# Every second weight piece of the experts issued from ScalarE's queue instead of SyncE's, with the overflow branch and the first preloaded pieces moved

## The chip, the cores and the metric

The kernel runs on one core of one Trainium2 chip. The metric is the device time of one execution in microseconds (us). TensorE (PE) multiplies, VectorE (DVE), ScalarE (ACT) and GpSimd (POOL) work elementwise, and SyncE (SP) does nothing but issue DMAs. Any of ACT, POOL and SP can issue a DMA. All matrices come from HBM as float32 and are read once: 418.78 MB in all.

## The reference

Two residual layers over 256 rows of 1024. The second ends in a top-2-of-8 expert SwiGLU, whose weights are most of the bytes (8 experts of 44 MB):

```python
def moe_swiglu(x, router, w_gate, w_up, w_down):
    logits = (t @ router).astype(jnp.float32)
    top_logits, top_idx = lax.top_k(logits, TOP_K)
    top_w = jax.nn.softmax(top_logits, axis=-1)
    ...
    for e in range(N_EXPERTS):
        out = out + gates[:, e:e + 1] * swiglu(t, w_gate[e], w_up[e], w_down[e])
```

The first layer (convolution, pooling, dense SwiGLU) and the first half of the second (short convolution, spatial gating) take 60 MB of weights.

## The kernel before, in words

Weights arrive in **pieces** ("chunks") of 1 MB, numbered in the order of use. The list `chunks` holds 57 pieces for everything ahead of the experts, then 336 for the experts. `raw_half` (L114) allocates a buffer and issues the piece's load the first time that it is asked for; the issue waits until the buffer's last reader is done. There are 8 general buffers (`raw`), and during a while some more that other data leave free (`AHEAD`, and the `whi` and `wlo` buffers by `IN_HI` and `IN_LO`, which name pieces by number).

The **experts** are taken by load: position 0 is a fixed expert, positions 1 to 7 are ranked on the chip, and their number is read into a register. Each position has a capacity in rows (`CAPS`): positions 1, 2 and 3 have 128 or more and are here called wide, the others 64 and are called plain. For wide positions each half of a piece is rounded by ACT into `whi` (L151) and the remainder is made by DVE into `wlo` (L158), both before PE may use it; PE then runs three passes. For plain positions PE multiplies by the raw piece itself. Position 1 has 32 rows beside its 128.

Each position runs through 7 **passes**; `STARTS` says in which pass it begins. Pass by pass the work is a list of **items**: gate, up and down of each position in the pass, two pieces each, so 6 pieces for each position in a pass. By `STARTS`, passes 0 to 3 and 25 to 27 hold one plain position, passes 4 to 10 and 18 to 24 one wide and one plain (12 pieces), and passes 11 to 17 one wide and two plain (18 pieces). In a pass of two or more the order is gates, then the downs of the pass before, then ups. Below, gW, dW and uW are the gate, down and up item of the wide position of such a pass, and gP, dP and uP those of the plain one: the order is gW gP dW dP uW uP.

The order on every engine is the order in which the code is written. `use` (L177) calls `prep`, which asks for the piece two ahead of the one that PE is to use (`LOOK_HI` = 4 halves). At an item's first step the results of the item before are taken from PSUM by ACT (`fdk`, `sgate`, L1298: a wait for PE) ahead of that. Because SP has no other work, it stands at a wait for a buffer and runs ahead of all other engines as far as there are free buffers.

Near the end, at item `end - IF_AT`, all engines read a flag and branch around code for rows over capacity (`over_capacity`, L1459), which isn't taken here. Ahead of it all pieces that are left have been asked for.

Of the kernel before, what the change touches and what calls it, by code (L numbers as in the profile page):

```python
# [8 lines left out]
F32 = mybir.dt.float32  # L9
# [8 lines left out]
P = 128  # L18
T = 256
# [4 lines left out]
NE = 8  # L24
# [8 lines left out]
RAW_BUFS = 8  # L33
WAIT = (6, 12, 6, 2)
CARRY = {(1, 0): 1, (1, 1): 2, (0, 0): 3, (0, 1): 3}
IF_AT = 5
CARRY_AT = 1
LAST_CUT = 2
AHEAD = {"ft": (0, 50), "fd": (15, 24), "fa": (2, 18), "fc": (3, 48), "fe": (7, 50), "fb": (8, 56), "f0": (9, 18), "f1": (10, 60)}

IN_HI, IN_LO = (16, 17, 18, -7, -6, -5), (19, 20, -4, -3)
TAIL, TAIL_HI, TAIL_LO = 12, 2, 1
RANK_AT = 3
FILL = (5, 2, 5, 4)
# [31 lines left out]
def tile_trunk(ctx: ExitStack, tc: tile.TileContext, a: dict, out: bass.AP, caps=CAPS, starts=STARTS,  # L76
               stop=None, dump=None):
    nc = tc.nc
    te, ve, se, pe_, sy = nc.tensor, nc.vector, nc.scalar, nc.gpsimd, nc.sync
# [21 lines left out]
    chunks, slot_pools = [], {"ra": rawp}  # L101
    raws, his, los, ahead = {}, {}, {}, {}
    state = {"use": 0}
# [7 lines left out]
    def block_chunk(w, r0, c0):  # L111
        chunks.append((lambda: w[r0:r0 + 512, c0:c0 + 512].rearrange("(k p) f -> p k f", p=P), 4, 512))

    def raw_half(n):  # L114

        c, h = divmod(n, 2)
        src, k, f = chunks[c]
        if c in ahead and ahead[c] in ("whi", "wlo"):
            if c not in raws:
                pool = hip if ahead[c] == "whi" else lop  # L120
                raws[c] = [pool.tile([P, k // 2, f], F32, name=ahead[c]) for _ in range(2)]
                for i, r in enumerate(raws[c]):
                    sy.dma_start(r, src()[:, i * k // 2:(i + 1) * k // 2, :])
            return raws[c][h]
        if c not in raws:
            tag = ahead.get(c, "raw")
            raws[c] = slot_pools[tag[:2]].tile([P, k, f], F32, name="raw", tag=tag)
            v = src()
            if c < FIRST_CUT:
                for i in range(2):  # L130
                    sy.dma_start(raws[c][:, :, i * P:(i + 1) * P], v[:, :, i * P:(i + 1) * P])
            elif c < len(chunks) - LAST_CUT:
                sy.dma_start(raws[c], v)
            else:
                for i in range(2):
                    sy.dma_start(raws[c][:, i * k // 2:(i + 1) * k // 2, :], v[:, i * k // 2:(i + 1) * k // 2, :])
        return raws[c][:, :, h * P:(h + 1) * P] if k == DB else raws[c][:, h * k // 2:(h + 1) * k // 2, :]

    spare = []
    made = {"hi": 0, "lo": 0}  # L140
# [55 lines left out]
    fg, fu, fd = a["even_ffn_w_gate"][0], a["even_ffn_w_up"][0], a["even_ffn_w_down"][0]  # L196
    o_in, o_out = a["odd_w_in"][0], a["odd_w_out"][0]
    mg, mu, md = a["odd_moe_w_gate"][0], a["odd_moe_w_up"][0], a["odd_moe_w_down"][0]
    eid_reg = {}
# [25 lines left out]
    n_moe = 2 * len(chunks)  # L225
# [7 lines left out]
    for c in range(max(c1 for _, c1 in AHEAD.values())):  # L233
        if c in IN_HI + IN_LO:
            continue
        tag = min((v[0], t) for t, v in held_by.items() if t == "raw" or AHEAD[t][0] <= c < AHEAD[t][1])[1]
        held_by[tag] = held_by[tag][1:] + [c]
# [13 lines left out]
    for p, n0 in starts:  # L251
        kept = [(m, k) for m, k in kept if m + NFB > n0]
        spills[p] = []
        for _, n in _blocks(caps[p]):
            k = 2 if n == P else 1
# [5 lines left out]
        plan.insert(len(plan) - 2, plan.pop(len(plan) - 5))  # L261

    def expert(p, w, r0, nr, c0, ncol):
        def src():
            if p and p not in eid_reg:
                eid_reg[p] = sy.value_load(ctli[0:1, p:p + 1], min_val=0, max_val=NE - 1)
            if p == 0:
                v = w[0, r0:r0 + nr, c0:c0 + ncol]
            else:
                v = w[bass.ds(eid_reg[p], 1), r0:r0 + nr, c0:c0 + ncol].rearrange("o r f -> (o r) f")  # L270
            return v.rearrange("(k p) f -> p k f", p=P)
        chunks.append((src, nr // P, ncol))

# [8 lines left out]

    for tag, cs in (("whi", IN_HI), ("wlo", IN_LO)):
        for c in cs:
            ahead[c + (n_moe // 2 if c > 0 else len(chunks))] = tag

    def stay_warm(n, w, m=None):

# [418 lines left out]
    for pair in range(2):  # L707
        for h in range(2):
            s = ws3(use())
# [14 lines left out]
    for q in range(4):  # L724
        w = use_plain() if PLAIN_B else use()
        for t in range(2):
            for j in range(2):
                k = 2 * q + j
# [15 lines left out]
    for g in range(4):  # L744
        o = bs[g // 2][:, (g % 2) * T:(g % 2 + 1) * T]
# [10 lines left out]
    for g in range(4):  # L756
        o = bs[g // 2][:, (g % 2) * T:(g % 2 + 1) * T]
# [100 lines left out]
    fe = ctx.enter_context(tc.tile_pool(name="fe", bufs=1, side="right"))  # L858
# [34 lines left out]
    fa = fy.tile([P, 2, 1024], F32, name="fa")  # L893
    fb = fy.tile([P, 2 * 1024 + 4], F32, name="fb")
    fc = fy.tile([P, 4, 512], F32, name="fc")
# [44 lines left out]
    for pair in range(2):  # L940
        for h in range(2):
            w = use()
            j = 2 * pair + h
            s = combine(ws_tile(w, x2T))
# [3 lines left out]
    for pair in range(2):  # L948
        for h in range(2):
            w = use()  # L950
            combine(ws_tile(w, x2T), vT[:, 2 * pair + h, :])
    for n in range(2):
# [3 lines left out]
        s = fc[:, 3, :]  # L956
# [7 lines left out]
    for pair in range(2):  # L964
        for h in range(2):
            w = use()
            j = 2 * pair + h
            s = combine(ws_tile(w, x2T))
# [7 lines left out]
    for pair in range(2):  # L976
        for h in range(2):
            w = use()
            j = 2 * pair + h
            s = combine(ws_tile(w, x2T))  # L980
# [92 lines left out]
    mop = ctx.enter_context(tc.tile_pool(name="mop", bufs=2, reuse_waits="tile"))  # L1073
# [25 lines left out]
    ctli = cst([P, NE + 1], "ctli", I32)  # L1099
# [122 lines left out]
    sgate, mh = {}, {}  # L1222
# [236 lines left out]
    def over_capacity():  # L1459

        R = total[0]
        flag = nc.values_load(ctli[0:1, NE:NE + 1], min_val=0, max_val=1)
        with tc.If(flag > 0):  # L1463
            capE, over = cst([P, NE], "capE"), cst([P, 2, NE], "over")
            c = small.tile([P, NE, NE], F32, name="bypos", bufs=1)
            ve.tensor_tensor(c, oh, capt[:, :, None].to_broadcast(sq), op=OP.mult)
            ve.tensor_reduce(capE, c.rearrange("p a e -> p e a"), axis=AX.X, op=OP.add)
            for t in range(2):
                ve.tensor_tensor(over[:, t, :], s1[:, t, :], capE, op=OP.is_gt)
            ve.tensor_tensor(over, over, gates, op=OP.mult)  # L1470
            xf = fx.tile([P, DB, T], F32, name="xf", tag="f0")
            for t in range(2):
                for q in range(2):
                    b = bank()
                    for k in range(4):
                        te.transpose(b[:, k * P:(k + 1) * P], X[:, t, (4 * q + k) * P:(4 * q + k + 1) * P], ident)
                    se.activation(xf[:, 4 * q:4 * q + 4, t * P:(t + 1) * P], b.rearrange("p (k f) -> p k f", k=4),
                                  AF.Copy)
            for e in range(NE):
                with tc.For_i(0, FE, P) as f0:  # L1480
                    wgu = fy.tile([P, 2, DB, P], F32, name="fbgu", tag="fc")
                    for i, w in enumerate((mg, mu)):
                        sy.dma_start(wgu[:, i], w[e][:, bass.ds(f0, P)].rearrange("(k p) f -> p k f", p=P))
                    wdt = fx.tile([P, D], F32, name="fbd", tag="f1")
                    sy.dma_start(wdt, md[e][bass.ds(f0, P), :])
                    bs = [bank(), bank()]
                    for i in range(2):
                        for k in range(DB):
                            mm(bs[i][:, :T], wgu[:, i, k, :], xf[:, k, :], k == 0, k == DB - 1)
                    s = mop.tile([P, T], F32, name="fbh", tag="mh", bufs=2)  # L1490
                    se.activation(s, bs[0][:, :T], AF.Silu)
                    ve.tensor_tensor(s, s, bs[1][:, :T], op=OP.mult)
                    for t in range(2):
                        for h in range(2):
                            sl = slice(h * 512, (h + 1) * 512)
                            b = bank()
                            mm(b, s[:, t * P:(t + 1) * P], wdt[:, sl], True, True)
                            ve.scalar_tensor_tensor(R[:, t, sl], b, over[:, t, e:e + 1], R[:, t, sl], op0=OP.mult,
                                                    op1=OP.add)
# [9 lines left out]
    for n, item in enumerate(plan):  # L1509
        if n == RANK_AT:  # L1510
            ranking()
        if n == total_at:
            start_total()
        if item in gathers:
            later(1, gather, *gathers[item])
        if n == end - IF_AT:
            drain()
            for c in range(made["hi"] // 2, len(chunks)):
                raw_half(2 * c)
            over_capacity()  # L1520
        if n == end - CARRY_AT:
            for (t, h), d in CARRY.items():
                if d < 4:
                    later(d, carry, t, h)
        if n >= end:
            drain()
        if n == len(plan) - 1:
            for (t, h), d in CARRY.items():
                if d >= 4:
                    later(d - 3, carry, t, h)  # L1530
        if item[0] == "d":
            down(*item[1:])
        else:
            project(*item)
# [19 lines left out]
    for t in range(2):  # L1554
        for h in range(2):
            nb = len(blocks[last])
            for bi in range(nb):
                if (t, h) not in F:
                    F[t, h] = bank()
                y, r = (ysum[last, bi][h], slice(0, P)) if blocks[last][bi][1] == P else \  # L1560
# [18 lines left out]
    for t in range(2):  # L1579
        for h in range(2):  # L1580
            r = y[:, t, half(h)]
# [33 lines left out]
```

## Time and profile before

| | us |
|---|---|
| median of 2 timed runs (1315.39 to 1319.24) | 1317.32 |
| the profiled execution | 1314.88 |
| its span, first to last instruction | 1313.2 |
| PE busy in it | 1256.2 |
| DVE busy | 713.5 |
| ACT busy | 514.5 |

The profiled execution lies 2.4 us under the median and 1.7 us over its own span. PE's busy time is modelled and counts pipelined matmuls, so a stage with a busy PE can still be one that waits for data. For that the DMA columns of the time slices are read.

### The profile page before, as it was taken

The page shows a single profiled execution, that of the slowest core. Times are in us where ns is not written, and L with a number is a line of the kernel's source. Part 1 is how long each engine was busy: PE and PEld are TensorE (multiplying, and loading weights), DVE is VectorE, ACT ScalarE, POOL GpSimd, SP SyncE. Part 2 cuts the span into 40 slices and gives each one's busy share as a digit, 9 for nine tenths or more (in the row PEclk, how much of TensorE's full clock was granted, in tenths as well). Part 3 has the DMA queues.
Part 4 walks back from the last instruction along what each step waited for, and adds up shares of the span by engine and source line. Part 5 has one row for each costly group of instructions (what it writes and reads, how often), then busy time and mean ns, then how long its engine had stood idle before and what let it go on. Part 6 is the DMA issues. An engine that isn't in the chain of part 4 may idle for free. (4 is left out here: it accounts for less than half of the span.)

```text
span 1313.2 us, 19384 instructions
## 1 busy us (share of the span) xinstructions
PE 1256.2 (96%) x7585; PEld 871.1 (66%) x7585; DVE 713.5 (54%) x1105; ACT 514.5 (39%) x726; POOL 32.0 (2%) x69
## 2 busy tenths in 40 slices
PE   7989999999999999999999999999999999999875
PEld 6848888888777666667765566565556567665541
DVE  4897676667984244655534334434435565564313
ACT  4246555546442144544432233332333244454200
POOL 5000000001000001000000000000000000000000
PEclk8999999999999999999999999999999999999988
DMA  8425755176875999999999999999999999999991
GB/s 293 166 70 176 256 184 182 65 253 194 323 271 185 393 393 394 394 392 393 393 393 371 381 397 374 364 380 391 392 397 396 394 393 395 393 394 394 393 393 76
DMA packets 195884, 421.17 MB, mean 321 GB/s; under 512 B 6896, under 2 KB 43448, under 8 KB 195784
## 3 DMA queue, kind: packets, MB, share of 16 engines
q1 hardware_dynamic: 194280, 414.58, 85.2%
q0 software_dynamic: 1504, 5.28, 1.1%
q8 instruction: 61, 1.00, 0.3%
q14 instruction: 39, 0.32, 0.1%
HBM read 418.78 MB, written 1.05 MB: 320 GB/s over the span
## 5 line engine op out<-in xcount | busy, mean ns | idle before, releaser
L158 DVE TENSOR_TENSOR wlo<-raw,whi 128x1024 fp32r<-128x1024 f32 x354 | 417.8, 1220 | 175.8 <-ACT whi L151 159.1
L151 ACT ACTIVATE whi<-raw 128x1024 fp32r<-128x1024 f32 x354 | 354.6, 1050 | 215.7 <-DMA raw<-in_odd_moe_w_up 99.1
L98 PE MATMUL mm<-whi,xgw 128*128 128x512 f32 x672 | 215.9, 403 | 0.4 <-DVE total L1431 0.4
L98 PEld LDWEIGHTS mm<-whi,xgw 128*128 128x128 f32 x672 | 122.0, 189 | 44.6 <-issue 13.3
L98 PE MATMUL mm<-raw,f1k 128*64 128x256 f32 (+1 forms) x1344 | 133.9, 384 | 0.0
L98 PE MATMUL mm<-wlo,xgw 128*128 128x512 f32 x336 | 131.9, 392 | 0.3 <-DVE wlo L158 0.3
L98 PE MATMUL mm<-big,whi 128*128 128x512 f32 (+1 forms) x448 | 129.2, 368 | 2.5 <-ACT whi L151 1.8
L98 PE MATMUL mm<-raw,fek 128*64 128x256 f32 x880 | 106.6, 390 | 7.3 <-DVEq L1463 6.7
L98 PE MATMUL acc<-whi,mh 128*128 128x512 f32 x336 | 106.3, 397 | 1.7 <-ACT whi L151 1.7
L98 PEld LDWEIGHTS mm<-raw,f1k 128*64 128x64 f32 (+1 forms) x1344 | 72.7, 127 | 52.2 <-issue 17.4
L1298 ACT ACTIVATE fdk<-mm 128x256 f32<-128x256 f32 (+1 forms) x49 | 23.2, 474 | 182.1 <-PE mm L98 181.9
L98 PE MATMUL mm<-big,wlo 128*128 128x256 f32 x384 | 92.7, 283 | 0.0
L98 PEld LDWEIGHTS mm<-raw,fek 128*64 128x64 f32 x880 | 61.1, 139 | 45.5 <-issue 19.0
L1301 DVE TENSOR_TENSOR fdk<-mm,fdk 128x256 f32<-128x256 f32 (+1 forms) x49 | 26.3, 537 | 118.5 <-PE mm L98 118.5
L98 PEld LDWEIGHTS mm<-big,whi 128*128 128x128 f32 x448 | 74.9, 192 | 14.2 <-ACT whi L151 2.0
L98 PE MATMUL acc<-raw,fbs 128*64 128x512 f32 (+1 forms) x528 | 84.0, 507 | 0.0
L98 PEld LDWEIGHTS acc<-whi,mh 128*128 128x128 f32 x336 | 61.4, 188 | 24.4 <-ACT whi L151 11.0
L98 PEld LDWEIGHTS mm<-wlo,xgw 128*128 128x128 f32 x336 | 63.5, 189 | 14.9 <-DVE wlo L158 0.7
L98 PEld LDWEIGHTS mm<-big,wlo 128*128 128x128 f32 x384 | 69.3, 192 | 3.7
L98 PE MATMUL acc<-wlo,mh 128*128 128x512 f32 (+1 forms) x176 | 67.8, 401 | 0.5 <-DVE wlo L158 0.5
L98 PEld LDWEIGHTS acc<-raw,fbs 128*64 128x64 f32 (+1 forms) x528 | 26.6, 125 | 47.9 <-issue 44.9
L98 PE MATMUL acc<-whi,ffh 128*128 128x512 f32 x176 | 55.6, 396 | 0.0
(292 smaller groups left out, 1315.7 us busy)
## 6 DMA issues: line engine op xcount, KB each, us to landing
raw<-in_odd_moe_w_gate SPq DMA_DIRECT2D x110, 1024.0 KB, 13.8
raw<-in_odd_moe_w_up SPq DMA_DIRECT2D x109, 1024.0 KB, 13.9
raw<-in_odd_moe_w_down SPq DMA_DIRECT2D x105, 1024.0 KB, 12.8
raw<-in_even_ffn_w_gate SPq DMA_DIRECT2D x11, 1024.0 KB, 5.6
raw<-in_even_ffn_w_up SPq DMA_DIRECT2D x11, 1024.0 KB, 8.3
raw<-in_even_ffn_w_down SPq DMA_DIRECT2D x11, 1024.0 KB, 7.0
raw<-in_odd_w_in SPq DMA_DIRECT2D x10, 1024.0 KB, 15.2
raw<-in_even_w_in SPq DMA_DIRECT2D x5, 1024.0 KB, 8.8
```

Of the source, the lines that this page charges most:

```text
L98: te.matmul(o, lhsT, rhs, start=start, stop=stop)
L151: se.activation(his[n], r, AF.Copy)
L158: ve.tensor_tensor(los[n], r, his[n].bitcast(F32), op=OP.subtract)
L1298: se.activation(s, v, AF.Silu)
L1301: ve.tensor_tensor(s, v, s, op=OP.mult)
```

## The change

- Pieces of the experts with an odd number (the first of each item's two, since the first expert piece is number 57) are issued by ACT (`se`) instead of SP. The order of the calls stays. Both engines read an expert's number into a register of their own.
- The branch is at 10 items ahead of the end instead of 5, and ahead of it pieces are asked for up to 8 past the one in use, not all that are left.
- Of the first pieces, 15 to 17 go to `whi` and 18 and 19 to `wlo` buffers (before: 16 to 18, and 19 and 20), the last pieces no longer use such buffers, and the buffer `fd` takes pieces from number 20 on instead of 15.
- A scratch tile in the branch's code shares another buffer.

```diff
-IF_AT = 5
+IF_AT = 10
...
-AHEAD = {"ft": (0, 50), "fd": (15, 24), ...
+AHEAD = {"ft": (0, 50), "fd": (20, 24), ...
-IN_HI, IN_LO = (16, 17, 18, -7, -6, -5), (19, 20, -4, -3)
+IN_HI, IN_LO = (15, 16, 17), (18, 19)
...
+    def raw_queue(c):
+
+        return se if c >= n_moe // 2 and c % 2 else sy
...
+                v = src()
                 for i, r in enumerate(raws[c]):
-                    sy.dma_start(r, src()[:, i * k // 2:(i + 1) * k // 2, :])
+                    raw_queue(c).dma_start(r, v[:, i * k // 2:(i + 1) * k // 2, :])
...
             elif c < len(chunks) - LAST_CUT:
-                sy.dma_start(raws[c], v)
+                raw_queue(c).dma_start(raws[c], v)
...
-            for c in range(made["hi"] // 2, len(chunks)):
+            for c in range(made["hi"] // 2, state["use"] // 2 + RAW_BUFS):
                 raw_half(2 * c)
```

ACT in a pass with one wide and one plain position, before: roundings (`whi`) and results taken from PSUM (`fdk` of 512 columns is the wide gate's, of 256 the plain gate's; `mh` is a transposed up).

```order
L435 ACTIVATE mh<-mm 128x4x128
L151 ACTIVATE whi<-raw 128x1024 x2
L1298 ACTIVATE fdk<-mm 128x512
L151 ACTIVATE whi<-raw 128x1024 x4
L1298 ACTIVATE fdk<-mm 128x256
L151 ACTIVATE whi<-raw 128x1024 x6
L435 ACTIVATE mh<-mm 128x4x128
```

The same place now, from the load of gP's first piece on; the ISA rows set the register for the address.

```order
L138 DMA raw<-in_odd_moe_w_gate 128x4x512
L1306 ACTIVATE fdk<-mm 128x512
L138 ISA
L138 DMA raw<-in_odd_moe_w_down 128x2x1024
L157 ACTIVATE whi<-raw 128x1024 x4
L1306 ACTIVATE fdk<-mm 128x256
L138 ISA
L138 DMA raw<-in_odd_moe_w_down 128x2x1024
L138 ISA
L138 DMA raw<-in_odd_moe_w_up 128x4x512
L157 ACTIVATE whi<-raw 128x1024 x4
```

The load of dW's first piece now stands behind the taking of the wide gate's result, and right ahead of the roundings of that same piece; the loads of dP's and uW's first pieces stand behind these and behind the plain gate's result.

SP from the third piece of position 0 on, before: both pieces of an item, one after the other.

```order
L133 DMA raw<-in_odd_moe_w_up 128x4x512 x2
L133 DMA raw<-in_odd_moe_w_gate 128x4x512 x2
L133 DMA raw<-in_odd_moe_w_up 128x4x512 x2
L133 DMA raw<-in_odd_moe_w_down 128x2x1024 x2
L133 DMA raw<-in_odd_moe_w_gate 128x4x512 x2
L133 DMA raw<-in_odd_moe_w_up 128x4x512 x2
L133 DMA raw<-in_odd_moe_w_down 128x2x1024 x2
L123 DMA whi<-in_odd_moe_w_gate 128x2x512 x4
```

ACT at the start of the experts now; `sgate` takes the result of position 0's gate from PSUM.

```order
L1306 ACTIVATE sgate<-mm 128x256
L138 DMA raw<-in_odd_moe_w_gate 128x4x512
L138 DMA raw<-in_odd_moe_w_up 128x4x512
L1306 ACTIVATE sgate<-mm 128x256
L138 DMA raw<-in_odd_moe_w_down 128x2x1024
L138 DMA raw<-in_odd_moe_w_gate 128x4x512
L138 DMA raw<-in_odd_moe_w_up 128x4x512
L1306 ACTIVATE sgate<-mm 128x256
L138 DMA raw<-in_odd_moe_w_down 128x2x1024
L128 DMA whi<-in_odd_moe_w_gate 128x2x512 x2
L128 DMA wlo<-in_odd_moe_w_up 128x2x512 x2
L1306 ACTIVATE sgate<-mm 128x256
```

The odd pieces of position 0 now stand behind the taking of PE's results, three after each gate; before, nothing of PE's expert work stood ahead of them on their queue but the buffers.

## Rows read from the trace of the kernel before

**Rows 1.** The page: 40 equal slices of the span, DMA busy tenths and rate.

```profile
DMA  8425755176875999999999999999999999999991
GB/s 293 166 70 176 256 184 182 65 253 194 323 271 185 393 393 394 394 392 393 393 393 371 381 397 374 364 380 391 392 397 396 394 393 395 393 394 394 393 393 76
```

**Rows 2.** Windows: stretch, length, busy PE, PEld, DVE, ACT, POOL, clock, DMA share, GB/s.

```profile
400.00:420.00 20.00, 20.00 (x170) 14.70 (x171) 12.06 (x41) 4.25 (x10) 0.00 (x0) 1.00 0.26 92
560.00:620.00 60.00, 60.00 (x343) 40.54 (x343) 33.33 (x37) 27.41 (x33) 0.00 (x0) 1.00 1.04 394
```

**Rows 3.** The page, costliest groups: DVE's and ACT's making of `wlo` and `whi`.

```profile
L158 DVE TENSOR_TENSOR wlo<-raw,whi 128x1024 fp32r<-128x1024 f32 x354 | 417.8, 1220 | 175.8 <-ACT whi L151 159.1
L151 ACT ACTIVATE whi<-raw 128x1024 fp32r<-128x1024 f32 x354 | 354.6, 1050 | 215.7 <-DMA raw<-in_odd_moe_w_up 99.1
```

**Rows 4.** Timeline of PE and ACT, one pass of a wide and a plain position.

```profile
574.85 3.67 PE L98 MATMUL mm<-raw,fek 128*64 128x256 f32 x32
578.45 0.73 PE L98 MATMUL acc<-whi,mh 128*128 128x512 f32 x2
...
584.11 3.65 PE L98 MATMUL acc<-raw,fbs 128*64 128x512 f32 x16
...
574.96 0.60 ACT L1298 ACTIVATE fdk<-mm 128x512 f32<-128x512 f32 x1 [6.17 <-PE mm L98]
...
582.68 2.01 ACT L151 ACTIVATE whi<-raw 128x1024 fp32r<-128x1024 f32 x2 [3.07 <-DMA raw<-in_odd_moe_w_up]
```

**Rows 5.** Timeline of PE, a gate item of position 1: first and last instructions.

```profile
765.07 1.07 PE L98 MATMUL mm<-raw,f1k 128*32 128x256 f32 x16
...
771.78 4.67 PE L98 MATMUL mm<-raw,f1k 128*32 128x256 f32 x48
```

**Rows 6.** Source line L133, SP's issues: ns min/median/max; landing over all of its pieces.

```profile
L133 SPq DMA_DIRECT2D raw<-in_even_ffn_w_gate x11: 367/368/368, 28.1 to 261.3; - x11
...
DMA to landing us min/median/max: 4.8/13.0/19.1
```

**Rows 7.** Source line L1540, two loads of 512 KB from POOL's queue beside SP's.

```profile
L1540 POOL DMA_DIRECT2D lnf<-in_odd_ln_g x1: 587/587/587, 992.5 to 992.5; - x1
L1540 POOL DMA_DIRECT2D lnf<-in_odd_ln_b x1: 531/531/531, 993.1 to 993.1; - x1
...
DMA to landing us min/median/max: 6.6/7.4/8.1
```

**Rows 8.** ACT's sequencer (ACTq) at the branch, and ACT's instruction ahead of it.

```profile
L1462 ACTq TENSOR_LOAD <-ctli x1: 467/467/467, 1260.4 to 1260.4; - x1
...
1260.42 0.39 ACT L1298 ACTIVATE fdk<-mm 128x256 f32<-128x256 f32 x1 [2.39 <-PE mm L98]
```

**Rows 9.** Timeline of SP, then of ACT, where the experts begin.

```profile
384.77 29.32 SPq L133 DMA_DIRECT2D raw<-in_odd_moe_w_down  x2
414.18 2.09 SPq L123 DMA_DIRECT2D whi<-in_odd_moe_w_gate  x4
...
429.48 0.39 ACT L1298 ACTIVATE sgate<-mm 128x256 f32<-128x256 f32 x1 [10.47 <-PE mm L98]
440.33 0.39 ACT L1298 ACTIVATE sgate<-mm 128x256 f32<-128x256 f32 x1 [10.47 <-PE mm L98]
```

**Rows 10.** Timeline of PE behind the branch.

```profile
1268.25 6.89 PE L98 MATMUL mm<-raw,fek 128*64 128x256 f32 x40 [6.75 <-DVEq L1463]
1275.07 0.44 PE L1308 MATMUL mm<-ident,fdk 128*128 128x128 f32 x2
```

More of the change, by code (lines that the diff above doesn't have):

```diff
@@ L35 @@
 CARRY = {(1, 0): 1, (1, 1): 2, (0, 0): 3, (0, 1): 3}
-IF_AT = 5
+IF_AT = 10
 CARRY_AT = 1
 LAST_CUT = 2
-AHEAD = {"ft": (0, 50), "fd": (15, 24), "fa": (2, 18), "fc": (3, 48), "fe": (7, 50), "fb": (8, 56), "f0": (9, 18), "f1": (10, 60)}
-IN_HI, IN_LO = (16, 17, 18, -7, -6, -5), (19, 20, -4, -3)
+AHEAD = {"ft": (0, 50), "fd": (20, 24), "fa": (2, 18), "fc": (3, 48), "fe": (7, 50), "fb": (8, 56), "f0": (9, 18), "f1": (10, 60)}
+IN_HI, IN_LO = (15, 16, 17), (18, 19)
 TAIL, TAIL_HI, TAIL_LO = 12, 2, 1
@@ L132, in raw_half @@
             elif c < len(chunks) - LAST_CUT:
-                sy.dma_start(raws[c], v)
+                raw_queue(c).dma_start(raws[c], v)
             else:
                 for i in range(2):
-                    sy.dma_start(raws[c][:, i * k // 2:(i + 1) * k // 2, :], v[:, i * k // 2:(i + 1) * k // 2, :])
+                    raw_queue(c).dma_start(raws[c][:, i * k // 2:(i + 1) * k // 2, :],
+                                           v[:, i * k // 2:(i + 1) * k // 2, :])
         return raws[c][:, :, h * P:(h + 1) * P] if k == DB else raws[c][:, h * k // 2:(h + 1) * k // 2, :]
@@ L263, in expert @@
     def expert(p, w, r0, nr, c0, ncol):
+        on = raw_queue(len(chunks))
         def src():
-            if p and p not in eid_reg:
-                eid_reg[p] = sy.value_load(ctli[0:1, p:p + 1], min_val=0, max_val=NE - 1)
+            if p and (p, on) not in eid_reg:
+                eid_reg[p, on] = on.value_load(ctli[0:1, p:p + 1], min_val=0, max_val=NE - 1)
             if p == 0:
@@ L269, in src @@
             else:
-                v = w[bass.ds(eid_reg[p], 1), r0:r0 + nr, c0:c0 + ncol].rearrange("o r f -> (o r) f")
+                v = w[bass.ds(eid_reg[p, on], 1), r0:r0 + nr, c0:c0 + ncol].rearrange("o r f -> (o r) f")
             return v.rearrange("(k p) f -> p k f", p=P)
@@ L284, in tile_trunk @@
         for c in cs:
-            ahead[c + (n_moe // 2 if c > 0 else len(chunks))] = tag
+            ahead[n_moe // 2 + c] = tag
     def stay_warm(n, w, m=None):
@@ L1489, in over_capacity @@
                             mm(bs[i][:, :T], wgu[:, i, k, :], xf[:, k, :], k == 0, k == DB - 1)
-                    s = mop.tile([P, T], F32, name="fbh", tag="mh", bufs=2)
+                    s = mop.tile([P, T], F32, name="fbh", tag="sgate", bufs=1)
                     se.activation(s, bs[0][:, :T], AF.Silu)
```

## The prediction

> **What bounds the kernel now.** I read the page's time slices first, then windows by stage, then the timeline of one pass on PE, ACT and SP. The reader is to see two halves. Up to about 420 us the DMA engines have room and PE sets the pace. From there to 1280 us they move 364 to 397 GB/s, mostly over 390 [rows 1]: 394 GB/s at a DMA share of 1.04 in the window from 560 us, while PE, too, counts as busy all the time [rows 2]. A piece of 1.049 MB so takes 2.67 us, and the passes last what their bytes last: 6 pieces 16 us, 12 pieces 32 us, 18 pieces 48 us. PE's own work is close under this. A wide item takes 5.7 us (578.45 to 584.11) and a plain one 3.7 us [rows 4], so a pass of both has 3 x 9.4 = 28 us; a gate of position 1 takes 765.07 to about 772.8, 7.7 us [rows 5], so a pass with it has 3 x (7.7 + 3.7 + 3.7) = 45 us.
>
> So no second queue can add bytes per second after 420 us. What it can do is to lose the lead. SP has the lead because it waits for nothing but buffers. ACT waits for PE: it sat idle 6.17 us for the wide gate's result before it took it, and 3.07 us for a landing before a rounding [rows 4].
>
> **The issue itself.** SP needs 0.37 us for one where its queue is not full [rows 6]. With ACT it is 168 issues, 62 us in all, beside 515 us of busy time, so ACT's sum of work bounds nothing. What counts is where each stands.
>
> Does a load on ACT's queue wait for what stands ahead of it there? The trace of before has no DMA on ACT. The nearest row is the branch: the read of the flag by ACT's sequencer starts at 1260.4, and the instruction ahead of it, which had waited 2.39 us for PE, at 1260.42 [rows 8]. So it came through when that wait ended, not earlier, and not after the instruction's 0.39 us either. I take it that a load on ACT waits for the *waits* ahead of it, not for the *work*.
>
> The Trainium skill says it otherwise (Perfetto Trace Analysis, DVE / Act Engine Instruction): the sequencer can fetch the next instruction as soon as one is pushed into the wait queue, so a load could be issued past roundings and results that still wait. By that rule the lead would mostly stay; that is rival A. The row above doesn't agree with it for the one control instruction that it shows.
>
> **How long a piece takes to land.** Alone 4.8 us, the least of all of SP's pieces [rows 6]. Beside SP's full queue, two loads of 512 KB from POOL's queue were issued at 992.5 and 993.1 and the later took 8.1 us, so this megabyte was there 8.7 us after its first issue [rows 7], less than the 13.0 us median on SP's own queue [rows 6]: another queue gets a share and doesn't stand behind SP's. Each further piece ahead of it on the same queue costs 2.67 us at the full rate and 5.3 us at half. So one piece lands in 4.8 to 8.7 us, the second of two in 7.5 to 14.0, the third of three in 10.1 to 19.3. Full rate holds when SP's buffers are all filled, half when SP always has something queued. SP is at most 8 buffers ahead and works in ACT's gaps as well, so I take a little under the middle: 6.5, 10 and 13 us.
>
> The Trainium skill (DMA: Bandwidth & Descriptors, Issuing engines are not separate DMA queues) states that loads from several engines interleave on the same 16 DMA engines, and that only issue time is saved. That speaks against a gain, and the 394 GB/s from one queue agree.
>
> **A pass of a wide and a plain position** (passes 4 to 10 and 18 to 24, 14 of them). I count from the landing of gW's first piece. ACT rounds it (1.05 us), DVE makes `wlo` (1.22 us) [rows 3], and PE starts at 2.3 and ends gW at 8.0. The load of gP's first piece went out shortly after 0 and is there in time. ACT then passes its wait for gW's result and issues dW's at 8.3; it lands at 14.8. The load of dP's, and behind it uW's, stand behind the rounding of dW's, which waits for that landing, and behind gP's result (8.0 + 3.7 = 11.7, earlier): out at 15.3. uW's lands 10 us later, 25.3. Behind its rounding go uP's and the next gW's: out at 25.8, landed at 35.8. So the pass lasts 8.3 + 6.5 + 10 + 10 + 1.0 for issues = 35.8 us instead of 32. PE, with 28 us of work, is never later than that. Ends: 8.3 + 4.8 + 7.5 + 7.5 + 1.0 = 29.1, under the 32 us that the bytes need, so no loss; and 8.3 + 8.7 + 14 + 14 + 1.0 = 46 us, 14 more. Sum: 14 x 3.8 = 53 us (0 to 196).
>
> **A pass with position 1 and two plain ones** (passes 11 to 17, 7 of them). From the landing of the wide gate: PE ends it at 10.0, the first plain gate at 13.7, and behind that result the wide down is issued at 13.9. One more plain piece is ahead of it, so it lands at 13.9 + 6.5 + 1 = 21.4. Both plain downs and the wide up go out by 22.5, and the up lands at 22.5 + 13 = 35.5. PE runs downs from 23.7 to 38.9 (7.7 + 3.7 + 3.7), then the wide up to 46.6. The last plain up and the next wide gate are issued behind that up's results, at 47 and 48.5 (the transposed up, `mh`, in between), and the gate lands at 48.5 + 6.5 + 1.5 = 56.5. Instead of 48 that is 8.5 us more; with the shortest landings 2.6, with the longest 19. Sum: 7 x 8.5 = 60 us (18 to 133).
>
> **The start of the experts.** Position 0 alone goes at PE's pace before, 440.33 - 429.48 = 10.85 us a pass [rows 9], faster than the 16 us that 6 pieces take, because SP had loaded some 20 pieces by then. ACT now has 3 odd pieces behind each gate's result. The first, a down, lands 6.5 us after the gate, while the up ahead takes PE only 3.7: some 3 us lost a pass, and the first gate of wide weights later by what ACT's list adds. I take 4 passes x 3 = 12 us (5 to 25; the top is ten odd pieces x 2.67 us, all the lead on ACT's side). The single-position passes at the end need 16 us for their bytes, and 1 + 6.5 + 2 x 3.7 us between a gate's result and the next gate's, so they lose nothing.
>
> **The moved pieces and the branch.** SP stood 29 us up to 414 us in two issues, the second a wait for the buffer `fd`, with `whi` pieces right behind [rows 9], at 92 GB/s [rows 2]. Piece 15 no longer waits for `fd`, which helps SP's side alone; I price it with the start above. The branch cost PE 6.75 us, in a stretch in which PE ran without a gap afterwards [rows 10]. At the start of pass 25 bytes are short, so most of the wait falls beside loads: 5 us won (7 won to 8 lost, if SP's and ACT's own halt at the branch empties the queues). The other buffer of the scratch tile is in code that isn't run: nothing.
>
> **Sum.** 1314.9 + 12 + 53 + 60 - 5 = 1435 us. The profiled execution lies 2.4 us under the median; I leave it at 1435.
>
> **Rivals.** *A: the lead stays.* ACT's sequencer goes past waiting results, or the shortest landings hold. Then a load on ACT stops only for the landing of a wide piece ahead of it, three times a pass, and the passes stay at 32 and about 50 us: 14 x 1 + 7 x 2 + 22 for the lost lead at the start - 5 = +45, 1360 us, and with the shortest landings throughout (0 + 18 + 5 - 7) 1331 us. For it: PE is idle little today, so there is slack for just-in-time loads; against it: the flag's read [rows 8]. *B: a load waits also for the work ahead of it,* or finds SP's queue mostly full. Four roundings (4 x 1.05) stand ahead of each of three issues on the path in a wide pass; 21 passes x 3 x some 2 us that nothing else hides = +126, 1560 us. For it: nothing in the trace excludes it for a load; against: the 0.39 us that the flag's read did not wait. *C: faster.* The mechanism is SP's wait at the start: with half of the pieces on another queue, a piece held up by its buffer no longer holds up those behind it, and the idle 20 us from 400 (92 of 393 GB/s, so 15 us of DMA time) are filled; it decides if ACT then keeps pace everywhere. With 6.75 us from the branch: 1315 - 22 = 1293 us. Against it: ACT's loads at that place stand behind `sgate` results that come only every 10.85 us [rows 9].
>
> **How the numbers follow.** The forecast has 0.62, A 0.19, B 0.14, C 0.05. About 2% (26 us, so under 1291 or over 1341) is what a measurement of this kernel can tell from no change. Faster by more: 0.03, since even C hardly reaches it. Within: 0.15, the lower part of A and most of C. Slower: 0.82. The sum's ends, all at once, are 1314.9 + 16 = 1331 and 1314.9 + 196 + 133 + 25 + 8 = 1677, but all ends at once are unlikely: landings can't all be long when the DMA engines have gaps. The range of 8 in 10 takes most of A and half of B: 1340 to 1560.
>
> **What would show it.** In the trace of the changed kernel: between 450 and 1250 us the rate is some 10% under 393 GB/s, with tenths of 8 in the DMA slices; ACT's landing waits ahead of `whi` grow from 159 us in DVE's column and PE shows real gaps ahead of wide items; ACT's loads start within 1 us of the `fdk` ahead of them; a wide and plain pass lasts about 36 us. If ACT's loads start while a result ahead of them still waits, A holds. If landings on ACT's queue are near 4.8 us, the sum is too high; if they are near 13 us, as on SP's today, it is far too low. The forecast is wrong altogether if the rate stays at 393 GB/s.

## The result, and the profile after

The changed kernel takes **1584.13 us** (1582.86 to 1585.41), 1.2045 times the time before, with an interval of 1.2013 to 1.2077: 267 us slower. The prediction had 1435 us and a range up to 1560, so its direction held and its size did not.

The page of the kernel after shows the same matmuls as before (7585), busy for longer, and DMA slices mostly with tenths of 6 to 8 where [rows 1] has nines. First the engine line, then the DMA lines of the 40 slices.

```profile
PE 1347.7 (85%) x7585; PEld 908.1 (57%) x7585; DVE 713.4 (45%) x1105; ACT 511.8 (32%) x726; POOL 31.8 (2%) x69
...
DMA  9137644576598887888778758686868979889983
GB/s 315 67 107 266 207 139 160 167 259 212 198 377 327 323 291 275 312 322 294 282 266 308 288 199 292 220 313 237 320 261 292 354 279 328 307 328 354 342 319 130
```

The reader is to see that no engine became full: TensorE is busy for 85% of the span, against 96% before, and the rate lies near 300 GB/s, against 393. The costliest groups of the page say what is waited for; they answer to [rows 3]. VectorE's wait for `whi` ahead of `wlo` is 428.3 us instead of 159.1. ScalarE's idle time ahead of `whi` is 485.8 us instead of 215.7, of which the landings of expert pieces are 441 us instead of 149 (gates, ups and downs added up):

```profile
L164 DVE TENSOR_TENSOR wlo<-raw,whi 128x1024 fp32r<-128x1024 f32 x354 | 417.6, 1222 | 450.4 <-ACT whi L157 428.3
L157 ACT ACTIVATE whi<-raw 128x1024 fp32r<-128x1024 f32 x354 | 352.0, 1048 | 485.8 <-DMA raw<-in_odd_moe_w_gate 152.5
```

To see where the time went, I cut both traces at the same events, ScalarE's takings of the 21 results of wide gates (`fdk` of 512 columns): up to the first one, the seven passes of wide and plain positions, the seven passes with position 1, the second block of six such intervals up to the last wide gate, and the rest. Columns: stretch, length, busy PE, PEld, DVE, ACT, POOL, clock, DMA share, GB/s. Before:

```profile
0.00:461.68 461.68, 441.08 (x2477) 357.32 (x2479) 316.71 (x628) 211.82 (x350) 25.00 (x63) 0.99 0.62 216
461.68:678.39 216.71, 214.97 (x1246) 146.63 (x1250) 113.45 (x122) 93.68 (x114) 5.89 (x4) 1.00 1.04 394
678.39:1015.90 337.51, 330.40 (x2390) 201.63 (x2394) 143.19 (x180) 111.80 (x146) 1.12 (x2) 1.00 1.02 384
1015.90:1210.00 194.10, 191.50 (x1040) 123.34 (x1041) 106.45 (x120) 78.44 (x92) 0.00 (x0) 0.99 1.04 394
1210.00:1313.20 103.20, 78.25 (x444) 42.13 (x444) 33.73 (x56) 18.77 (x25) 0.00 (x0) 0.92 0.77 292
```

After:

```profile
0.00:476.83 476.83, 446.22 (x2475) 357.77 (x2475) 317.18 (x628) 211.52 (x350) 24.85 (x63) 0.97 0.60 207
476.83:754.42 277.59, 234.43 (x1246) 154.60 (x1250) 112.71 (x122) 92.88 (x114) 5.88 (x4) 0.93 0.85 306
754.42:1237.80 483.38, 382.50 (x2411) 226.03 (x2411) 142.79 (x179) 111.24 (x147) 1.11 (x2) 0.88 0.75 275
1237.80:1471.00 233.20, 203.18 (x1017) 126.77 (x1017) 107.04 (x121) 77.61 (x94) 0.00 (x0) 0.94 0.90 322
1471.00:1583.70 112.70, 81.37 (x444) 42.96 (x444) 33.63 (x56) 18.51 (x25) 0.00 (x0) 0.90 0.71 262
```

The lengths grow by 15.1, 60.9, 145.9, 39.1 and 9.5 us, in all 270.5. TensorE's busy time takes 91.5 us of that (5.1, 19.5, 52.1, 11.7, 3.1), and its idle time 179 us. (21 of the 2411 matmuls of the position-1 stretch, about 3 us, fell behind the cut before.) More than half of the whole lies in the seven passes with position 1: 69.1 us each (483.38 / 7) instead of 48.2.

**One pass of a wide and a plain position**, ScalarE and its sequencer (ACTq), from a wide gate's landing to the next:

```profile
655.56 2.00 ACT L157 ACTIVATE whi<-raw 128x1024 fp32r<-128x1024 f32 x2 [8.80 <-DMA raw<-in_odd_moe_w_gate]
...
667.24 0.60 ACT L1306 ACTIVATE fdk<-mm 128x512 f32<-128x512 f32 x1 [6.04 <-PE mm L98]
667.38 0.38 ACTq L138 DMA_DIRECT2D raw<-in_odd_moe_w_down  x1
672.69 1.06 ACT L157 ACTIVATE whi<-raw 128x1024 fp32r<-128x1024 f32 x1 [4.85 <-DMA raw<-in_odd_moe_w_down]
673.08 0.38 ACTq L138 DMA_DIRECT2D raw<-in_odd_moe_w_down  x1
673.63 0.38 ACTq L138 DMA_DIRECT2D raw<-in_odd_moe_w_up  x1
...
681.35 1.06 ACT L157 ACTIVATE whi<-raw 128x1024 fp32r<-128x1024 f32 x1 [4.50 <-DMA raw<-in_odd_moe_w_up]
...
682.27 0.40 ACTq L138 DMA_DIRECT2D raw<-in_odd_moe_w_gate  x1
...
689.71 2.01 ACT L157 ACTIVATE whi<-raw 128x1024 fp32r<-128x1024 f32 x2 [4.46 <-DMA raw<-in_odd_moe_w_gate]
```

This is the chain that the prediction wrote down, link by link: the down is issued 0.14 us after ScalarE gets past its wait for the gate's result, the up behind the rounding of the down, the next gate behind the rounding of the up. Each issue starts while ScalarE still works on the instruction ahead (673.08 inside a rounding of 672.69 to 673.75), so it waits for waits, not for work. On the statement in the Trainium skill (Perfetto Trace Analysis, DVE / Act Engine Instruction) that the sequencer is free as soon as an instruction is pushed into the wait queue, the trace disagrees for these loads: the down at 667.38 did not go out during the 6.04 us in which the result ahead of it waited.

**One pass with position 1**, the same engine, from landing to landing:

```profile
1009.18 1.06 ACT L157 ACTIVATE whi<-raw 128x1024 fp32r<-128x1024 f32 x1 [10.82 <-DMA raw<-in_odd_moe_w_gate]
...
1027.84 0.38 ACT L1306 ACTIVATE fdk<-mm 128x256 f32<-128x256 f32 x1 [2.31 <-PE mm L98]
1027.99 0.38 ACTq L138 DMA_DIRECT2D raw<-in_odd_moe_w_down  x1
1037.80 2.00 ACT L157 ACTIVATE whi<-raw 128x1024 fp32r<-128x1024 f32 x2 [9.57 <-DMA raw<-in_odd_moe_w_down]
...
1040.67 0.38 ACTq L138 DMA_DIRECT2D raw<-in_odd_moe_w_up  x1
...
1055.73 1.06 ACT L157 ACTIVATE whi<-raw 128x1024 fp32r<-128x1024 f32 x1 [13.77 <-DMA raw<-in_odd_moe_w_up]
...
1066.34 0.38 ACTq L138 DMA_DIRECT2D raw<-in_odd_moe_w_gate  x1
1078.17 1.06 ACT L157 ACTIVATE whi<-raw 128x1024 fp32r<-128x1024 f32 x1 [11.38 <-DMA raw<-in_odd_moe_w_gate]
```

It takes 69.0 us (1078.17 - 1009.18); the prediction had 56.5. Behind the gate's landing the down is issued after 18.8 us instead of 13.9, the largest single difference. Two more timelines of that place, TensorE's and VectorE's, show where it arises:

```profile
1006.85 3.38 PE L98 MATMUL mm<-raw,f1k 128*64 128x256 f32 x24
1014.49 0.44 PE L1316 MATMUL mm<-ident,fdk 128*128 128x128 f32 x2 [4.26 <-DVE fdk L1309]
1014.85 1.93 PE L98 MATMUL mm<-raw,f1k 128*32 128x256 f32 x16
```

```profile
1010.27 1.23 DVE L164 TENSOR_TENSOR wlo<-raw,whi 128x1024 fp32r<-128x1024 f32 x1 [9.06 <-ACT whi L157]
...
1011.75 2.35 DVE L164 TENSOR_TENSOR wlo<-raw,whi 128x1024 fp32r<-128x1024 f32 x2
1014.01 0.42 DVE L1309 TENSOR_TENSOR fdk<-mm,fdk 128x256 f32<-128x256 f32 x1
```

TensorE was done with the item before at 1010.23, but VectorE took that item's result only at 1014.01, behind three `wlo` of the late gate, and TensorE's transpose waited for it. So the gate begins at 1014.85, 5.7 us after the landing and not 2.3, and its first 16 matmuls take 1.93 us, where the same took 1.07 before [rows 5]; the granted clock is 0.56 from 1014.40 to 1018.20.

The pass behind it, from 1078.17 on, takes 68.0 us. There, too, the gate begins late, 5.9 us after its landing, and at half speed, and the down is issued 20.2 us after that landing:

```profile
1084.10 1.94 PE L98 MATMUL mm<-raw,f1k 128*32 128x256 f32 x16
...
1098.37 0.38 ACTq L138 DMA_DIRECT2D raw<-in_odd_moe_w_down  x1
1108.87 3.90 ACT L157 ACTIVATE whi<-raw 128x1024 fp32r<-128x1024 f32 x4 [10.27 <-DMA raw<-in_odd_moe_w_down]
...
1126.26 1.06 ACT L157 ACTIVATE whi<-raw 128x1024 fp32r<-128x1024 f32 x1 [13.22 <-DMA raw<-in_odd_moe_w_up]
...
1146.14 1.06 ACT L157 ACTIVATE whi<-raw 128x1024 fp32r<-128x1024 f32 x1 [6.35 <-DMA raw<-in_odd_moe_w_gate]
```

### The profile page after: what moved, and what is told of

It reads as the page before. It is cut to its first block, busy times and chain, and to the rows that moved or that the text cites. A ratio compares the mean times of both kernels' runs of the same rounds, so it can differ in the third digit from the quotient of the medians.

```text
span 1583.7 us, 19226 instructions
## 1 busy us (share of the span) xinstructions
PE 1347.7 (85%) x7585; PEld 908.1 (57%) x7585; DVE 713.4 (45%) x1105; ACT 511.8 (32%) x726; POOL 31.8 (2%) x69
## 5 line engine op out<-in xcount | busy, mean ns | idle before, releaser
L164 DVE TENSOR_TENSOR wlo<-raw,whi 128x1024 fp32r<-128x1024 f32 x354 | 417.6, 1222 | 450.4 <-ACT whi L157 428.3
L157 ACT ACTIVATE whi<-raw 128x1024 fp32r<-128x1024 f32 x354 | 352.0, 1048 | 485.8 <-DMA raw<-in_odd_moe_w_gate 152.5
L98 PE MATMUL mm<-whi,xgw 128*128 128x512 f32 x672 | 222.0, 412 | 5.7 <-ACT whi L157 4.1
L98 PE MATMUL mm<-raw,f1k 128*64 128x256 f32 (+1 forms) x1344 | 156.2, 426 | 41.5 <-DMA raw<-in_odd_moe_w_gate 22.7
L98 PE MATMUL acc<-whi,mh 128*128 128x512 f32 (+1 forms) x344 | 125.1, 457 | 48.1 <-ACT whi L157 48.0
L98 PEld LDWEIGHTS mm<-whi,xgw 128*128 128x128 f32 x672 | 126.3, 196 | 53.2 <-issue 13.5
L98 PEld LDWEIGHTS mm<-raw,f1k 128*64 128x64 f32 (+1 forms) x1344 | 82.6, 140 | 103.6 <-issue 73.9
L98 PE MATMUL mm<-wlo,xgw 128*128 128x512 f32 x336 | 136.0, 405 | 4.2 <-DVE wlo L164 4.2
L98 PE MATMUL mm<-raw,fek 128*64 128x256 f32 x896 | 111.8, 398 | 17.3 <-DMA raw<-in_odd_moe_w_gate 10.5
L98 PE MATMUL acc<-raw,fbs 128*64 128x512 f32 (+1 forms) x560 | 101.0, 548 | 23.2 <-DMA raw<-in_odd_moe_w_down 23.2
L98 PEld LDWEIGHTS acc<-whi,mh 128*128 128x128 f32 (+1 forms) x344 | 73.0, 220 | 77.0 <-ACT whi L157 58.9
L98 PE MATMUL acc<-wlo,mh 128*128 128x512 f32 x168 | 75.8, 451 | 5.0 <-DVE wlo L164 4.7
```

The lines of the kernel that those rows point to most:

```text
L98: te.matmul(o, lhsT, rhs, start=start, stop=stop)
L157: se.activation(his[n], r, AF.Copy)
L164: ve.tensor_tensor(los[n], r, his[n].bitcast(F32), op=OP.subtract)
```

## The experiments

Theory T, after the result: a load on ScalarE's queue goes out only when ScalarE has got past every wait ahead of it, for landings and for TensorE's results; so it comes late, and TensorE waits for it. Rivals: the issues cost ScalarE's time (I); a second queue is bad by itself (Q); the moves beside it cost the time; only the waits for landings count (L). Diffs are against the changed kernel. The ratios are against the kernel before, run on the same chip.

**The moves alone (moves_sp).**

```diff
-        return se if c >= n_moe // 2 and c % 2 else sy
+        return sy
```

> All pieces stay on SyncE's queue; only the moved first pieces and the moved branch are kept. Theory T (a load on ScalarE's queue stands in line behind that engine's waits, so the lead is lost): 1305 to 1318 us, 393 GB/s from 430 us on, and the 6.75 us that PE stood at the branch partly won. Rival M (the moved pieces or the branch cost the time): over 1400 us.

1309.65 us, ratio 0.9948 (0.9923 to 0.9972). So the moves are not at fault; they gain a little, and this is the one version that beats both kernels, the one before by half a per cent. SyncE's wait at the start is shorter (it stood 29.32 us in two issues, [rows 9]); its longest there is 14.70 us in four:

```profile
388.58 14.70 SPq L128 DMA_DIRECT2D whi<-in_odd_moe_w_gate  x4
```

TensorE's wait behind the branch, in its own timeline, is what it was, 6.78 us against 6.75 [rows 10]:

```profile
1238.64 8.69 PE L98 MATMUL mm<-raw,fek 128*64 128x256 f32 x64 [6.78 <-PEq L1471]
```

**The second queue on an engine without such waits (second_on_pool).**

```diff
-        return se if c >= n_moe // 2 and c % 2 else sy
+        return pe_ if c >= n_moe // 2 and c % 2 else sy
```

> The odd pieces go on GpSimd's queue instead of ScalarE's; all else as in the changed kernel. GpSimd takes no results from PE and waits for no landing of pieces. Theory T: the lead stays, 1305 to 1350 us. Rival Q (two queues that share the DMA engines are slower, or pieces land later, whichever engine issues): 1500 us or more, with landings of 7 us and a rate near 300 GB/s.

1317.59 us, ratio 1.0009 (0.9964 to 1.0055). The same 168 pieces from GpSimd's queue cost nothing that can be measured against the kernel before, and gain nothing. Against the moves alone (1309.65) they may cost up to 8 us, 0.6%. Rival Q falls: what costs is whose queue it is. That nothing is gained either agrees with the Trainium skill (DMA: Bandwidth & Descriptors, Issuing engines are not separate DMA queues). Nor do the landings make the difference. From the page's DMA issues, with KB each and the median of issue to landing, a gate's piece on GpSimd's queue takes 10.0 us, longer than the 8.5 us of the same pieces on ScalarE's queue in the changed kernel:

```profile
raw<-in_odd_moe_w_gate POOLq DMA_DIRECT2D x55, 1024.0 KB, 10.0
```

**More distance (act_lead2, act_lead4, act_lead5).** Everything stays on its queue, but pieces are asked for `LEAD` pieces earlier than the two of the changed kernel.

```diff
+LEAD = 4
...
+            if state["use"] >= n_moe:
+                for c in range(n // 2, min(n // 2 + LEAD, len(chunks) - 1) + 1):
+                    raw_half(2 * c)
             r = raw_half(n)
```

> Odd pieces on ScalarE's queue as in the changed kernel, but each piece is asked for 4 pieces earlier in the program (6 ahead of its use instead of 2), so that its load stands ahead of the waits of two items. Theory T: most of the 267 us come back, 1310 to 1400 us. Rival Q, and rival I (the issues themselves cost ScalarE the time): no change, 1560 to 1600 us, since as many loads go on the same queues.

> The changed kernel with each piece asked for two pieces earlier (four ahead of its use, not two); everything stays on its queue. Theory T (the loads come late by what ScalarE waits for ahead of them; a piece more of distance gives about 2.7 to 3.4 us of cover): the loss of 274 us on 1309.65 falls step by step with the distance, from 274 at two to 37 at six pieces; at four a stall of one wait (4 to 10 us) is mostly covered and a chain of several is not: 1390 to 1470 us. Rival S (the wait for the next result holds the load whatever the distance, until a threshold): below 1370 or above 1540 us.

> The same with five pieces earlier (seven ahead, with eight buffers). Theory T (distance covers the waits): the 37 us that were left at four earlier shrink to 0 to 30, 1310 to 1340 us. Rival I (what was left is ScalarE's time for the issues, 0.38 us each, in front of its conversions): no further gain, 1340 to 1355 us. Rival B (the eight buffers now set the time of a load): as I, or slower than 1355 us.

With 2, 4 and 5 pieces more: 1433.11 us (ratio 1.0886, 1.0814 to 1.0958), 1347.23 (1.0235, 1.0197 to 1.0272) and 1322.96 (1.0042, 1.0023 to 1.0061). The loads, their number, size, engine and issue time are those of the changed kernel; only the distance differs (of the pieces on both queues), and it brings back 261 of the 267 us. All three times lie in the ranges of theory T. So the loss is lateness. Rival I could hold 13 us at the most, the distance of 1322.96 from the moves alone. TensorE's longest waits in the trace with 5 (line, for what, us in all, times, longest) have no landing of an expert's piece among them; the only one in the whole view is 0.6 us long:

```profile
PE mm L1320 <- DVE fdk L1313: 13.7, 10, 2.4
PE mm L99 <- PEq L1475: 6.9, 1, 6.9
```

In the changed kernel that view reads:

```profile
PE acc L98 <- ACT whi L157: 48.0, 13, 7.3
PE acc L98 <- DMA raw<-in_odd_moe_w_down: 35.5, 15, 5.3
PE mm L98 <- DMA raw<-in_odd_moe_w_gate: 35.0, 8, 8.1
PE mm L1316 <- DVE fdk L1309: 29.6, 13, 4.3
```

**The load ahead of the result, not behind it (act_ahead).** The distance stays two pieces.

```diff
     def step():
 
-        tick()
         n = state["use"]
+        raw_half(min(n + LOOK_HI, 2 * len(chunks) - 1))
+        tick()
```

> The odd pieces stay on ScalarE's queue and are asked for at the same distance of two pieces, but each load is written ahead of the projection result (fdk) that falls due in the same step, not behind it. Theory T (a load on ScalarE stands behind every wait ahead of it, and the waits for TensorE's results are the larger part): the wait that stood right ahead is gone for the loads that follow a result, the waits for landed neighbours stay: 1380 to 1460 us, and the loads begin well before the result's start. Rival L (only the waits for landed pieces hold the loads, the results cost nothing): 1540 to 1584 us.

1479.56 us, ratio 1.1249 (1.1176 to 1.1322): 105 us less than the changed kernel, and 20 above the top of what T had put down. The loads go out as meant; here one stands 5.6 us ahead of the result that it followed before, and behind another wait, of 0.70 us:

```profile
640.50 0.39 ACT L1091 ACTIVATE fak<-mm 128x256 fp32r<-128x256 f32 x1 [0.70 <-PE mm L1221]
640.64 0.38 ACTq L138 DMA_DIRECT2D raw<-in_odd_moe_w_down  x1
646.22 0.60 ACT L1307 ACTIVATE fdk<-mm 128x512 f32<-128x512 f32 x1 [5.34 <-PE mm L98]
```

So the waits for the results just ahead are worth some 105 us, and rival L, that only landings hold the loads, falls. But they are not the larger part that T had claimed: 170 of the 274 us (against the moves alone) stay, with the waits for landings and the other results.

**Only a part of the pieces (act_plain, act_wide).** On ScalarE's queue are the odd pieces of positions without a 128-row block (105 of 168), or of those with one (63).

```diff
-        return se if c >= n_moe // 2 and c % 2 else sy
+        return se if c >= n_moe // 2 and c % 2 and not wide[c] else sy
...
+        wide[len(chunks)] = any(n == P for _, n in _blocks(caps[p]))
```

(act_wide has `and wide[c]`.)

> Only the odd pieces of plain positions (105 of 168) go on ScalarE's queue; wide ones stay on SyncE's. No load is then followed by a wait for its own landing, only preceded by waits for PE's results. Theory T with the landing waits as the larger part: 1340 to 1430 us. Rival I: loss by count, 105/168 of 267 us, 1480 us.

> Only the odd pieces of the positions with a 128-row block (63 of 168) are on ScalarE's queue, the rest on SyncE's: the counterpart of the run that had only the plain positions' 105 there (1480.98 us, +171 on 1309.65). If the two parts add up: 1309.65 + 274 - 171 = about 1413 us (1390 to 1435), to which a count of pieces leads as well (63/168 x 274 = 103). Rival (one late piece in a pass already costs the pass what two cost it): 1450 to 1510 us. Rival L (waits for landed pieces that ScalarE converts are all of it; these are found in wide positions alone): above 1540 us.

Plain ones alone: 1480.98 us, ratio 1.1251 (1.1204 to 1.1297). Wide ones alone: 1526.66, ratio 1.1607 (1.1556 to 1.1658). Theory T's range for the first is missed, and so is every range for the second. Rival I's 1480 us for the first is hit, but by luck: by the same count the second would have lost 103 us, and it lost 217. Against the moves alone they lose 171 and 217 us, 388 together, where both at once lose 274; and 63 wide pieces cost 3.4 us each, 105 plain ones 1.6. The loss doesn't go by the count. It fits that a late piece stops the pass and that a second late one in the same pass then costs less, which these two runs suggest but don't show. That is the direction of the rival written for act_wide, though the time lies 17 us above its range.

**TensorE kept busy in the gaps (act_warm, with moves_warm as its control).** Dummy matmuls stand ahead of the items of positions with a 128-row block; in the control all loads are on SyncE's queue.

```diff
+FILLERS = 20
...
         kinds = [n for _, n in blocks[p]]
+        if P in kinds:
+            fill = bank()
+            for _ in range(FILLERS):
+                mm(fill[:, :P], ident, ident, True, True)
```

> The changed kernel with 20 dummy matmuls of 128 columns, whose result nothing reads, ahead of each of the 63 items of the positions with a 128-row block, so that TensorE works in a part of the gaps in which it waits for a late piece. Theory K (a part of the loss is TensorE's lower granted clock behind such gaps: busy time 1347.7 against 1256.2 us for the same matmuls): the clock rises above 0.929, and the time stays below 1584 us or within 20 us of it although work is added. Rival N (the clock is a by-product and costs nothing): the time grows by at least what the same dummies add where nothing is on ScalarE (the run beside this one).

> The control of the run before it: the same 20 dummy matmuls ahead of the 63 items, with every load on SyncE's queue. Its distance from 1309.65 us is what the dummies cost by themselves where TensorE has few gaps. Estimate: 1260 matmuls of some 0.05 to 0.1 us are 63 to 126 us of TensorE, of which a part lies beside transfers: 1330 to 1420 us.

1713.09 us (ratio 1.3024, 1.2955 to 1.3094) and 1579.01 (1.2005, 1.1953 to 1.2057). The dummies were dearer than estimated, 297.6 us of TensorE in the control (each of the 1260 stands as two matmuls in the trace):

```profile
L99 PE MATMUL mm<-ident 128*128 128x128 f32 x2520 | 297.6, 277 | 0.0
```

They cost 269 us on SyncE's queue and 129 on ScalarE's, so both K (under 20) and N (at least 269) miss: about half of the dummies' time fell into gaps. Without the dummies TensorE's own work is 1580.6 - 297.8 = 1282.8 us in act_warm, against 1347.7 in the changed kernel: with the gaps partly filled, the same matmuls run 65 us shorter, at a mean clock of 0.963 instead of 0.929. Some of that may come of the subtraction: in the control it gives 1535.7 - 297.6 = 1238.1 us, 17 under the 1254.7 of the moves alone. How much of the 267 us the clock caused can't be read from the pair, since the control is bound by TensorE (1535.7 of 1577.6 us busy), and that hides late loads as well.

**ScalarE's queue without the moves (queue_only).** Branch, first pieces and the two buffers (`fd`, `fbh`) as in the kernel before; of the diff two places are shown.

```diff
-IF_AT = 10
+IF_AT = 5
...
-IN_HI, IN_LO = (15, 16, 17), (18, 19)
+IN_HI, IN_LO = (16, 17, 18, -7, -6, -5), (19, 20, -4, -3)
```

> Half of the change: the odd pieces on ScalarE's queue, but the branch, the first pieces and the two buffers where they stood in the kernel before. If the two halves add up, as the moves alone were worth -5.6 us: 1584 + 6 = about 1590 us (1578 to 1602). Rival (the moves cost time beside ScalarE's late loads, since first pieces and tail were placed for loads that come in order): 1540 to 1578 us.

1578.00 us (1571.59 to 1584.41, two runs), ratio 1.1986 (1.1854 to 1.2119). The interval is 35 us wide and holds the changed kernel's ratio, and it reaches into the ranges of both expectations. That the queue alone makes the loss is shown; whether the moves help or harm beside it is not.

## Why the prediction was right in direction and wrong in size

| term of the sum | predicted, us | measured, us |
|---|---|---|
| start of the experts | +12 (5 to 25) | +15.1 |
| 14 passes of wide and plain | +53 (0 to 196) | 60.9 + 39.1 = +100.0 (13 intervals) |
| 7 passes with position 1 | +60 (18 to 133) | +145.9 |
| branch, moved pieces, tail | -5 (-7 to +8) | +9.5 |
| sum | +120 | +270.5 |

**Right: the mechanism.** That a load on ScalarE waits for the waits ahead of it, taken from the one flag read of [rows 8], is what 667.24 and 667.38 show, and the distance runs confirm that lateness is the loss. Rival A (the sequencer goes past a waiting result) is out: the load at 667.38 did not. Rival C (faster) is out too. Its mechanism is there in the moves alone, where 313 GB/s instead of 92 [rows 2] flow from 400 to 420 us, but the first wide gate's result comes only 0.6 us earlier (461.06 against 461.68). Rival B named 1560 us, the nearest of all, but its conditions are not what the runs show. Loads don't wait for ScalarE's work (673.08). And over all loads on ScalarE's queue an expert's piece lands in 7.1 us (median, 4.8 to 14.9), not in the 13.0 us of SyncE's own queue before [rows 6]; on GpSimd's queue longer landings cost nothing.

**Right in kind: what would show it.** The loads shown start within 0.15 us of the `fdk` ahead. One wide and plain pass takes 34.15 us against the 35.8 of the chain, though their mean is 39.7 us in the first block. The rate was to be 10% under 393 GB/s; it is 18 to 30% under (306, 275 and 322 in the windows).

**Failed: the size of the position-1 passes**, the step "PE ends it at 10.0, the first plain gate at 13.7, and behind that result the wide down is issued at 13.9", and what follows from it up to "and the gate lands at 48.5 + 6.5 + 1.5 = 56.5. Instead of 48 that is 8.5 us more". It is the largest error, 146 against 60, and above the term's own worst case. The two passes shown, link by link:

| link | predicted, us | from 1009.18 | from 1078.17 |
|---|---|---|---|
| the gate's landing to the down's issue | 13.9 | 18.8 | 20.2 |
| to the down's landing | 7.5 | 9.8 | 10.5 |
| to the up's landing | 14.1 | 17.9 | 17.4 |
| to the next gate's landing | 21.0 | 22.4 | 19.9 |
| sum | 56.5 | 69.0 | 68.0 |

The first link is the furthest off in both. The prediction had the gate begin 2.3 us after its landing and run at full speed; it began after 5.7 and 5.9 us, and its beginning ran at a granted clock of 0.56 and 0.50 (1084 to 1090 us). In between lies a wait that the prediction didn't name: VectorE runs in order as well, and took a finished result behind the `wlo` of the late gate, so that TensorE's transpose stood for 4.26 and 2.79 us. In all passes such waits of TensorE rose only from 11.0 us, in 9, to 29.6, in 13 (the first pass shown has the longest), so they are a smaller part of the whole. The landings of down, up and next gate, taken "a little under the middle" as 7.5, 13 and 8.0, came to 9.8, 15.1 and 11.8 us in the first pass, which is 8.2 of its 12.5 us, but to 10.5, 13.0 and 6.8 in the second, 1.8 of 11.5.

**Failed: TensorE at full speed**, the step "PE, with 28 us of work, is never later than that", and the 7.7 and 3.7 us per item everywhere. These came from a stretch with a granted clock of 1.00 [rows 2], and the sum put a slower TensorE behind gaps at nothing. In the changed kernel the same matmuls take 91.5 us more, 19.5 + 11.7 in the wide and plain blocks and 52.1 in the position-1 block. The idle time alone grew by 41.4 + 27.4 = 68.8 us in the 13 intervals of wide and plain passes, 5.3 each where 3.8 were foreseen, and by 93.8 us in the 7 of position 1, 13.4 each where 8.5 were. So the waits came out some 40 to 60% above their price, and the slower work comes on top of that. The busy time is from the trace; that filled gaps shorten it, by 65 us, is from act_warm; its share of the time itself stays open.

**The moves and the branch.** The moves alone are worth 0.5%, as the term said, but not where it said: the branch's wait stayed at 6.78 us. Of the 4.9 us between the two profiled executions (1313.2 and 1308.3), 0.6 lie ahead of the first wide gate's result and 2.1 behind the last one's, so which of the moves gains them is not shown. With ScalarE's late loads the tail lost 9.5 us.

**The range.** It left out the sum's upper ends because "all ends at once are unlikely". The rows above suggest that they are not independent: a late load makes a gap, behind it the clock is lower, the slower item gives a later result, and the result holds the next load. No run separates these steps.

## What to carry to other kernels

A load belongs on a queue whose engine never waits for what the load feeds: the same 168 pieces cost at most 0.6% on GpSimd's queue and 20% on ScalarE's, whose instructions wait for TensorE. If it must be there, its distance has to cover the waits ahead of it: two pieces gave 1584 us, seven gave 1323. And when a change opens gaps ahead of TensorE, the work behind the gaps is not to be priced at the durations of a stretch without any.

## What the runs showed of the hardware

TensorE's granted clock fell with gaps of a few microseconds. Here are the ends of two gaps, of 6.11 us and, in the pass shown above, of 2.99 us, each with the stretch behind it:

```profile
935.80 3.68 PE L98 MATMUL mm<-S,tok 128*128 128x64 f32 x16 [6.11 <-ACT f1k L1177]
936.00:944.00 8.00, 7.90 (x38) 5.48 (x38) 3.52 (x6) 2.41 (x4) 0.00 (x0) 0.55 0.39 126
...
673.80 1.22 PE L98 MATMUL acc<-whi,mh 128*128 128x512 f32 x2 [2.99 <-ACT whi L157]
673.80:680.60 6.80, 6.76 (x16) 4.83 (x17) 4.61 (x4) 3.05 (x4) 0.00 (x0) 0.52 1.04 402
```

0.55 and 0.52 are close to the lower of the two levels, 1.2 GHz; from 944 to 952 us and from 680.6 to 690 us the clock is 1.00 again, which is 2.4. In the last stretch a down item of the wide position begins, which takes 5.7 us in the kernel before [rows 4] and here from 673.80 to 682.8, 9.0 us: so behind the gap of 3 us the item took another 3 us longer.

An issue on GpSimd takes longer than one on ScalarE, 0.75 us against 0.38 (medians), and this played no part: the engine has next to nothing else to do there, and its loads stand behind no wait for a result of TensorE.
